# Row factors over partitions by two DMAs instead of matmuls with ones, and a square root moved ahead of a scaling, in a hybrid HGRN2 / RG-LRU layer

## Chip, cores and metric

The kernel runs on one core of a Trainium2 chip. The metric is the device time of one launch in microseconds (us); the median over the runs is given with its lowest and highest value, and one further execution was taken with the hardware profiler. All shapes are float32; many matmul operands are float32r, the packed form in which TensorE multiplies float32 in one pass.

## What is computed

One layer on x of shape (2048, 1024), cut from the reference:

```
xn    = rms_norm(x, mix_norm_w)                 # x / sqrt(mean(x^2) + 1e-6) * w, per row
proj  = xn @ w_in                               # 1024 -> 6 groups of 512 columns
o_hg  = hgrn2(q, f, i, g)                       # 4 heads, chunked gated recurrence
o_lru = rglru(conv(lru_x), lru_gate)            # real-gated linear recurrence
h     = x + concat(o_hg, o_lru) @ w_out         # 1024 -> 1024, "output projection"
hn    = rms_norm(h, ffn_norm_w)
h     = h + (silu(hn @ w_gate) * (hn @ w_up)) @ w_down     # 1024 -> 2816 -> 1024
out   = rms_norm(h, final_norm_w)
```

## The kernel before

**Halves and tiles.** The 2048 rows are done in two halves of 1024, each of two chunks `c` of 512 rows, each of four row tiles `tt` of 128. `KT` is 8 (slices of 128 of the 1024 features), `TPC` is 4, `CW` is 512. Matmul operands are kept as a pair: a rounded "hi" part, made by ScalarE (ACT), and the rest, "lo", made by VectorE (DVE) as a subtraction; three matmuls (hi·hi, hi·lo, lo·hi) stand for one product. So each operand costs a cast on ACT and a subtraction on DVE (`split`, lines 234 and 170 of the profile).

**The second half's input.** In `norm_steps(c)` (lines 621 to 651) the second half's chunk c is normalised while the first half's output projection runs. It has three kinds of steps. Four `stat` steps load row tiles of x and sum their squares on ACT; the last calls `factor`, which makes `rs`, a tile of 128 partitions by 4, with one POOL instruction (L559): the row factors 1/sqrt(mean + eps), a row in a partition. `spread` brings these 512 factors into a tile `row` of 128 partitions by 512, the same 512 numbers in every partition, since the transposed x (`xk`, features in partitions, rows in the free dimension) needs a factor per column. Before, it does so in `row_spread`: four times DVE scales the identity by a column of `rs` (L590, tile `dg`), and TensorE multiplies ones by it (L591, tile `tpb`, in PSUM); ACT copies the result to SBUF (L639). Eight `apply` steps each load a slice `xk` of the transposed x, multiply it on DVE by the weight and by `row` (L646), and split it into `xn` hi and lo.

**The output projection.** It is a seven-product scheme over 2x2 blocks, in the order p1, p2, p6, p5, p7, p3, p4 (`OORDER`). Each product has four row tiles with 12 matmuls each, 48 in all (line 1311), left operands `mx_a`, `mx_b`, `mx_f`, `mx_e`, `mx_g`, `mx_c`, `mx_d`, and two weight tiles `raw_o` loaded by SP and split into `whi_o` and `wlo_o`. The `raw` pool has three buffers, so the load of a weight tile waits until the `wlo` subtraction of the tile three before it has read its buffer. `prepare` makes the next product's left operand on ACT and DVE: sums `s1`, `s2` and differences of `hg` and `y` (line 1237), then `split`. After each row tile DVE adds the bank in PSUM to the residual (`res`, line 1316).

**What sets the order.** The norm steps are hung at numbered slots of the projection: slot 4·i + tt is run after row tile tt of product i; statistics sit at slots -4 to 3, `spread` of chunk c at slot 8 + c, `apply` at 12 + 8·c and on. Within what dependencies allow, the tile framework's scheduler then fixes the order on each engine at build time; on the chip each engine takes its instructions in that order. Buffers come from rotating pools: `xin` (4) holds the x tiles and then `xk`, `late` (5) holds `dg`, `row` and others.

**The end.** In the last product of the last half (p4 of the down projection, lines 1088 to 1091) each row tile g is finished as soon as its sum is there: `square` sums its second half's squares on ACT (L937), takes the root on ACT (L942) and the reciprocal on DVE (L943); `finish` scales one half of the columns on DVE (L957), the other on ACT (L958), and stores both, from SP and, for the last tile, also from ACT's queue (L959, L960).

Of the kernel before, what the change touches and what calls it, by code (L numbers as in the profile page):

```python
# [8 lines left out]
F32 = mybir.dt.float32  # L9
F32R = mybir.dt.float32r  # L10
AF = mybir.ActivationFunctionType
ALU = mybir.AluOpType

P = 128
# [11 lines left out]
TPC = CW // P  # L26
NTT = T // P
# [10 lines left out]
def hybrid_layer(ctx: ExitStack, tc: tile.TileContext, x, x_t, norm_w, cols, w_in, gate_w, w_out, w_gu, w_down, out):  # L38
    nc = tc.nc
# [4 lines left out]
    dram = ctx.enter_context(tc.tile_pool(name="dram", bufs=1, space=bass.MemoryType.DRAM))  # L44
# [7 lines left out]
    def xin(nm):  # L52
        return sb.tile([P, CW], F32, tag="xin", name=nm, bufs=4)


    def block(nm, dt=F32R):
        return sb.tile([P, 4, CW], dt, tag="bt", name=nm, bufs=14)
# [7 lines left out]
    def late(nm):  # L65
        return sb.tile([P, CW], F32, tag="late", name=nm, bufs=5)
# [4 lines left out]
    def aux(nm):  # L71
        return psp.tile([P, CW], F32, tag="aux", name=nm)
# [12 lines left out]
        out=tri[:, 0:P], in_=tri[:, 0:P], pattern=[[1, P]], compare_op=ALU.is_ge, fill=0.0, base=0, channel_multiplier=-1  # L85
# [145 lines left out]
    def split(dst, src, scale=None):  # L231
        if scale is None:
            ins = nc.scalar.copy(out=dst[0], in_=src)  # L233
            v.tensor_tensor(out=dst[1], in0=src, in1=f(dst[0]), op=ALU.subtract)
        else:
            ins = nc.scalar.activation(out=dst[0], in_=src, func=AF.Copy, scale=scale)
            v.scalar_tensor_tensor(out=dst[1], in0=src, scalar=scale, in1=f(dst[0]), op0=ALU.mult, op1=ALU.subtract)
        return ins

    def act_tile(nm):  # L240
        return [[block(f"{nm}_{s}{n}") for n in range(2)] for s in range(2)]

    def part(xt, s, k, ts=slice(0, CW)):
        return xt[s][k // 4][:, k % 4, ts]
# [301 lines left out]
    def chain(ins, behind):  # L546
        tc.add_manual_dep(
            ins.ins,
            behind.ins.name,
            mybir.DependencyInfo(mybir.DependencyClass.NoSync, mybir.DependencyReason.DATA),  # L550
            reason="order",
        )
# [3 lines left out]
    def factor(sums, nm):  # L556
        rs = small.tile([P, 4], F32, tag="ss", name="ss_" + nm, bufs=8)
        v.scalar_tensor_tensor(out=rs, in0=sums[0], scalar=EPS, in1=sums[1], op0=ALU.add, op1=ALU.add)
        nc.gpsimd.tensor_tensor(out=rs, in0=rs, in1=mhalf, op=ALU.pow)  # L559
        return rs  # L560
# [21 lines left out]
                    v.tensor_tensor(out=lo[:, ks], in0=raw[i][:, ks], in1=f(hi[:, ks]), op=ALU.subtract)  # L582
        return xw

    def row_spread(c, rs, nm="x0"):
        nm = f"{nm}_{c}"
        pbc, dg = aux("tpb" + nm), late("dg" + nm)
        for tt in range(TPC):
            ts = slice(tt * P, (tt + 1) * P)
            v.tensor_scalar(out=dg[:, ts], in0=ident, scalar1=rs[:, tt : tt + 1], scalar2=None, op0=ALU.mult)  # L590
            nc.tensor.matmul(pbc[:, ts], lhsT=ones.broadcast_to([P, P]), rhs=dg[:, ts], start=True, stop=True)  # L591
        return pbc
# [28 lines left out]
    def norm_steps(c):  # L621
        box = {}
        sums = []

        def stat(tt):
            if tt == 0:
                sums.extend(small.tile([P, 4], F32, tag="ss", name=f"ss{n}_x1_{c}", bufs=8) for n in range(2))
            r0 = T + c * CW + tt * P
            for n in range(2):
                p = xin(f"x1_{c}_{tt}_{n}")  # L630
                nc.sync.dma_start(out=p, in_=x[r0 : r0 + P, n * CW : (n + 1) * CW])
                nc.scalar.activation(out=p, in_=p, func=AF.Square, scale=1.0 / 32.0, accum_out=sums[n][:, tt : tt + 1])
            if tt == TPC - 1:
                box["rs"] = factor(sums, f"x1_{c}")

        def spread():
            pbc = row_spread(c, box["rs"], "x1")
            box["row"] = late(f"row1_{c}")
            nc.scalar.copy(out=box["row"], in_=pbc)  # L639

        def apply(k):
            if k == 0:
                box["xn"] = act_tile(f"xn1_{c}")
            p = xin(f"xk1_{c}_{k}")
            nc.sync.dma_start(out=p, in_=x_t[k * P : (k + 1) * P, T + c * CW : T + (c + 1) * CW])
            v.scalar_tensor_tensor(  # L646
                out=p, in0=p, scalar=par[:, C_NW + k : C_NW + k + 1], in1=box["row"], op0=ALU.mult, op1=ALU.mult
            )
            split([part(box["xn"], s, k) for s in range(2)], p)

        return box, [lambda tt=tt: stat(tt) for tt in range(TPC)], spread, [lambda k=k: apply(k) for k in range(KT)]


    def tt_(out, a, b, op, e=None):
        (e or v).tensor_tensor(out=out, in0=a, in1=b, op=op)  # L655
# [217 lines left out]
    def residual(half):  # L873
        hp = [[page(f"hd{half}_{g}_{n}") for n in range(2)] for g in range(NTT)]
        return hp
# [5 lines left out]
    def down_plain(half, c, fs, hp, extra, ahead=()):  # L881
# [38 lines left out]
        for tt in range(TPC):  # L920
            finish(half, c * TPC + tt, hp[c * TPC + tt])
# [4 lines left out]
    def final_row(half, g):  # L926
        if g not in fin:
            fin[g] = wvec(2, f"wfin{half}_{g}") if g % TPC == 0 else fin[g - 1]
        return fin[g]

    def square(half, g, n, p):
        first = (half, g) not in sums_f
        if first:
            sums_f[half, g] = small.tile([P, 4], F32, tag="sf", name=f"sf{half}_{g}", bufs=8)
        ss = sums_f[half, g]
        junk = late(f"jf{half}_{g}_{n}")
        nc.scalar.activation(out=junk, in_=p, func=AF.Square, scale=1.0 / 32.0, accum_out=ss[:, n : n + 1])  # L937
        if first:
            v.tensor_scalar(out=ss[:, 2:3], in0=ss[:, n : n + 1], scalar1=EPS, scalar2=None, op0=ADD)
            tt_(p, p, final_row(half, g)[:, n * CW : (n + 1) * CW], MUL)  # L940
        else:
            nc.scalar.activation(out=ss[:, 3:4], in_=ss[:, n : n + 1], func=AF.Sqrt, bias=ss[:, 2:3])  # L942
            v.reciprocal(out=ss[:, 3:4], in_=ss[:, 3:4])  # L943

    def finish(half, g, hp, n=None):
        row = final_row(half, g)
        r0 = half * T + g * P
        if n is None:
            rs = rstd_of(hp, f"f{half}_{g}")
            for n in range(2):  # L950
                nsl = slice(n * CW, (n + 1) * CW)
                v.scalar_tensor_tensor(out=hp[n], in0=hp[n], scalar=rs, in1=row[:, nsl], op0=MUL, op1=MUL)
                nc.sync.dma_start(out=out[r0 : r0 + P, nsl], in_=hp[n])
            return
        rs = sums_f[half, g][:, 3:4]
        nsl, osl = slice(n * CW, (n + 1) * CW), slice((1 - n) * CW, (2 - n) * CW)
        v.scalar_tensor_tensor(out=hp[n], in0=hp[n], scalar=rs, in1=row[:, nsl], op0=MUL, op1=MUL)  # L957
        nc.scalar.activation(out=hp[1 - n], in_=hp[1 - n], func=AF.Copy, scale=rs)  # L958
        nc.sync.dma_start(out=out[r0 : r0 + P, nsl], in_=hp[n])  # L959
        (nc.scalar if g == NTT - 1 else nc.sync).dma_start(out=out[r0 : r0 + P, osl], in_=hp[1 - n])  # L960

    fin = {}

# [141 lines left out]
    for half in range(2):  # L1107
# [3 lines left out]
        if half == 0:  # L1111
            warm_up()
            raw, xs, rows = first_loads()
            xw, rs = [], []
# [59 lines left out]
        for s in range(8):  # L1174
# [6 lines left out]
            for c in range(NC):  # L1181
                k = 2 * (NC * s + c)
                nm = f"{half}_{s}_{c}"
# [13 lines left out]
                else:  # L1197
                    d = {"pre": lru_pre(i, pa, pb, nm)}
                    g = k + 3 if c == 0 else k + 2
# [5 lines left out]
        def at_slot(i, *fs):  # L1205
            fill.setdefault(i, []).extend(fs)

        if half == 0:
            for c in range(NC):
                nb, stats, spread, applies = norm_steps(c)  # L1210
                boxes.append(nb)
                for j, f_ in enumerate(stats):
                    at_slot(-4 + 4 * c + j, f_)
                at_slot(8 + c, spread)
                for j, f_ in enumerate(applies):
                    at_slot(12 + 8 * c + j, f_)
        else:
            bops[0], steps, last = acts(hn_d[0], "0", False)
            for j, f_ in enumerate(steps[0]):
                at_slot(12 + j, f_)  # L1220
            for j, f_ in enumerate(steps[1]):
                at_slot(min(20 + j, 27), f_)
# [17 lines left out]
        for c in range(NC):  # L1240
# [11 lines left out]
            t = block(f"hg{half}_{c}", F32)  # L1252
            hg.append(t)
            for tt in range(TPC):
                tp = transposed(tt, 0, vts[c][:, tt, :], f"o{half}_{c}_{tt}")
                nc.scalar.activation(
                    out=t[:, :, tt * P : (tt + 1) * P], in_=tp, func=AF.Copy, scale=par[:, C_HN : C_HN + 1]
# [34 lines left out]
        for i, name in enumerate(OORDER):  # L1292
# [9 lines left out]
            c, n = to[name]  # L1302
            if i in (1, 2, 5):
                residual_in(*to[OORDER[i + 1]])
            for tt in range(TPC):
# [8 lines left out]
                g = c * TPC + tt  # L1314
                p = res[g, n]
# [63 lines left out]
    for half in range(2):  # L1379
        ffn_up(half, bops[half], later if half == 0 else ())  # L1380
        hp = residual(half)
# [87 lines left out]
```

## Time and profile before

| | |
|---|---|
| median of 3 runs | 2073.01 us (2072.82 to 2073.02) |
| the profiled execution | 2072.78 us, of which the span from first to last instruction is 2071.1 us |
| TensorE clock granted | 0.999 of full speed |
| busy: TensorE / weight loads / DVE / ACT / POOL | 99% / 83% / 75% / 49% / 3% of the span |
| DMA | 279.60 MB, 135 GB/s on the mean; every transfer is issued by SP but two, which ACT issues; none by POOL |

PE is TensorE's matmuls and PEld its weight loads. Matmuls are pipelined: a busy time of one is longer than the step from one start to the next. In a timeline each row has the start, the duration, engine, line, operation, out<-in, the count, and in brackets the idle time ahead of it and what ended it; instructions of one line that follow each other are merged. In a list of waits the columns are total time, times and the longest. Numbers at the end of tile names are left out in the profile.

### The profile page before, as it was taken

How to read it: one execution, taken by the hardware profiler on the slowest of the kernel's cores; microseconds unless marked ns; L12 is line 12 of the kernel's file. 1: busy time of each engine (PE TensorE's matmuls, PEld its weight loads, DVE VectorE, ACT ScalarE, POOL GpSimd, SP SyncE). 2: the span in 40 equal slices, each digit the busy share in tenths (PEclk: the TensorE clock that was granted, in tenths of full speed). 3: DMA queues.
4: the chain of work that ended last, by engine and by line, in shares of the span. 5: the costliest groups of instructions: out<-in, count | busy, mean ns of one | idle time of the engine just before them, and what ended most of it. 6: DMA issues, size and time to landing. Idle time of an engine off the chain costs nothing.

```text
span 2071.1 us, 26057 instructions
## 1 busy us (share of the span) xinstructions
PE 2059.6 (99%) x9570; PEld 1710.8 (83%) x9570; DVE 1555.1 (75%) x2517; ACT 1021.6 (49%) x1698; POOL 68.8 (3%) x97
## 2 busy tenths in 40 slices
PE   9999999999999999999999999999999999999998
PEld 8888887888888888888888888888888888888887
DVE  7878758836888599667667578779776676669787
ACT  7677776456777554343343354245333333344334
POOL 1011110000000000000000000001000000000000
PEclk9999999999999999999999999999999999999999
DMA  7322227841111364433433384356332232266424
GB/s 265 101 78 79 69 77 244 299 123 41 41 41 42 104 231 148 148 127 117 142 127 128 112 303 139 122 162 196 110 118 92 96 129 94 85 247 238 156 85 142
DMA packets 148351, 279.60 MB, mean 135 GB/s; under 512 B 12288, under 2 KB 28672, under 8 KB 148224
## 3 DMA queue, kind: packets, MB, share of 16 engines
q1 hardware_dynamic: 147936, 277.66, 39.5%
q8 instruction: 75, 1.23, 0.2%
q14 instruction: 52, 0.43, 0.1%
q10 hardware_dynamic: 288, 0.29, 0.0%
HBM read 210.53 MB, written 67.37 MB: 134 GB/s over the span
## 4 chain that ended last, share of the span: by engine, by line
PE 96%; ACT 1%; DVE 1%; DMA 1%; issue 0%; POOL 0%; ACTq 0%; DVEq 0%
PE quad_e L771 12%; PE quad_g L771 12%; PE quad_a L771 12%; PE pda L1055 10%; PE pdb L1055 7%; PE quad_f L771 6%; PE pox L1311 4%; PE pa L261 3%; PE pb L262 3%; PE pa L263 3%; PE pb L263 3%; PE pa L262 3%; PE pb L261 3%; PE poyp L1311 3%; PE pv L615 2%; PE pd L911 1%
## 5 line engine op out<-in xcount | busy, mean ns | idle before, releaser
L771 PE MATMUL quad_e<-act_c,wgu_c 128*128 128x512 f32 x528 | 128.7, 391 | 0.0
L771 PE MATMUL quad_e<-act_e,wgu_e 128*128 128x512 f32 x528 | 127.5, 389 | 0.0
L771 PE MATMUL quad_f<-act_f,wgu_f 128*128 128x512 f32 x528 | 127.5, 389 | 0.0
L771 PE MATMUL quad_g<-act_g,wgu_g 128*128 128x512 f32 x528 | 127.5, 389 | 0.0
L771 PE MATMUL quad_a<-act_a,wgu_a 128*128 128x512 f32 x528 | 127.5, 390 | 0.0
L771 PE MATMUL quad_a<-act_b,wgu_b 128*128 128x512 f32 x528 | 127.1, 390 | 0.3 <-ACT e L808 0.3
L771 PE MATMUL quad_g<-act_d,wgu_d 128*128 128x512 f32 x528 | 127.2, 390 | 0.0
L771 PEld LDWEIGHTS quad_a<-act_b,wgu_b 128*128 128x128 f32 x528 | 99.2, 188 | 21.1 <-ACT e L808 0.6
L771 PEld LDWEIGHTS quad_a<-act_a,wgu_a 128*128 128x128 f32 x528 | 99.2, 188 | 20.7 <-ACT wgu_a L233 0.3
L771 PEld LDWEIGHTS quad_g<-act_g,wgu_g 128*128 128x128 f32 x528 | 99.2, 188 | 20.5
L771 PEld LDWEIGHTS quad_f<-act_f,wgu_f 128*128 128x128 f32 x528 | 99.2, 188 | 20.5
L771 PEld LDWEIGHTS quad_e<-act_e,wgu_e 128*128 128x128 f32 x528 | 99.2, 188 | 20.5
L771 PEld LDWEIGHTS quad_g<-act_d,wgu_d 128*128 128x128 f32 x528 | 99.2, 188 | 20.3
L771 PEld LDWEIGHTS quad_e<-act_c,wgu_c 128*128 128x128 f32 x528 | 99.2, 188 | 20.2
L655 DVE TENSOR_TENSOR u<-u,quad_g 128x512 f32<-128x512 f32 x88 | 60.3, 686 | 59.2 <-PE quad_g L771 59.2
L261 PE MATMUL pa<-xn,whi_in 128*128 128x512 f32 x256 | 101.0, 395 | 0.0
L263 PE MATMUL pa<-xn,whi_in 128*128 128x512 f32 x256 | 100.7, 394 | 0.0
L262 PE MATMUL pb<-xn,wlo_in 128*128 128x512 f32 x256 | 100.6, 393 | 0.0
L263 PE MATMUL pb<-xn,whi_in 128*128 128x512 f32 x256 | 100.6, 393 | 0.0
L262 PE MATMUL pa<-xn,wlo_in 128*128 128x512 f32 x256 | 100.5, 393 | 0.0
L261 PE MATMUL pb<-xn,whi_in 128*128 128x512 f32 x256 | 100.2, 391 | 0.0
L293 ACT ACT_TABLE_LOAD x74 | 94.9, 1283 | 2.5 <-PEq L1458 1.2
(379 smaller groups left out, 4893.5 us busy)
## 6 DMA issues: line engine op xcount, KB each, us to landing
raw<-in_w_gu SPq DMA_DIRECT2D x88, 512.0 KB, 3.8
raw_in<-in_w_in SPq DMA_DIRECT2D x47, 512.0 KB, 4.2
ao_p<-as SPq DMA_DIRECT2D x76, 256.0 KB, 2.5
xk<-in_x_t SPq DMA_DIRECT2D x32, 256.0 KB, 5.3
x<-in_x SPq DMA_DIRECT2D x32, 256.0 KB, 4.5
res<-in_x SPq DMA_DIRECT2D x32, 256.0 KB, 6.2
raw_o_p<-wo_p SPq DMA_DIRECT2D x16, 512.0 KB, 4.7
h<-res SPq DMA_DIRECT2D x32, 256.0 KB, 4.0
```

Source lines behind the costliest of these rows:

```text
L261: nc.tensor.matmul(ps, lhsT=whi[:, ks], rhs=hi, start=(k == 0), stop=False)
L262: nc.tensor.matmul(ps, lhsT=wlo[:, ks], rhs=hi, start=False, stop=False)
L263: nc.tensor.matmul(ps, lhsT=whi[:, ks], rhs=lo, start=False, stop=(k == KT - 1))
L293: in_line(lambda: nc.scalar.preload_act_table(func))
L615: ins = nc.tensor.matmul(banks[tt], lhsT=a, rhs=w, start=(k + i == 0), stop=(k == KT - 1 and i == 2))
L655: (e or v).tensor_tensor(out=out, in0=a, in1=b, op=op)
L771: nc.tensor.matmul(ps, lhsT=w[:, s, ks], rhs=x, start=first and k + n == 0, stop=k == 3 and n == 2, skip_group_check=not first)
L911: nc.tensor.matmul(ps, lhsT=a[:, 1, tsl], rhs=whi[:, nsl], start=False, stop=(i == len(fs) - 1))
L1055: nc.tensor.matmul(ps, lhsT=x, rhs=y, start=first and q + n == 0, stop=q == gr.n - 1 and n == 2, skip_group_check=not first)
L1311: nc.tensor.matmul(ps, lhsT=x_, rhs=y_, start=first and q + m == 0, stop=q == 3 and m == 2, skip_group_check=not first)
```

## The change

Two parts. In `norm_steps`, `spread` no longer calls `row_spread`: POOL issues a DMA that writes the 128 x 4 factors, transposed, as 4 x 128 into DRAM (512 elements of 4 bytes), and then a DMA that reads these 512 numbers back into every partition of `row`. The `spread` slots become 4 and 6 in place of 8 and 9. In the end part, ACT's scaling of a tile's other half (and its store) is held back until the next tile's root is on ACT, and ordered behind it.

```diff
-    def row_spread(c, rs, nm="x0"):
-        nm = f"{nm}_{c}"
-        pbc, dg = aux("tpb" + nm), late("dg" + nm)
+    def row_spread(c, rs):
+        pbc, dg = aux(f"tpbx0_{c}"), late(f"dgx0_{c}")
...
         def spread():
-            pbc = row_spread(c, box["rs"], "x1")
+            d = dram.tile([TPC, P], F32, name=f"rs1_{c}")
             box["row"] = late(f"row1_{c}")
-            nc.scalar.copy(out=box["row"], in_=pbc)
+            nc.gpsimd.dma_start(out=d.rearrange("t p -> p t"), in_=box["rs"])
+            nc.gpsimd.dma_start(out=box["row"], in_=d.rearrange("t p -> (t p)").partition_broadcast(P))
...
-            nc.scalar.activation(out=ss[:, 3:4], in_=ss[:, n : n + 1], func=AF.Sqrt, bias=ss[:, 2:3])
+            roots[half, g] = nc.scalar.activation(out=ss[:, 3:4], in_=ss[:, n : n + 1], func=AF.Sqrt, bias=ss[:, 2:3])
...
-        nc.scalar.activation(out=hp[1 - n], in_=hp[1 - n], func=AF.Copy, scale=rs)
         nc.sync.dma_start(out=out[r0 : r0 + P, nsl], in_=hp[n])
-        (nc.scalar if g == NTT - 1 else nc.sync).dma_start(out=out[r0 : r0 + P, osl], in_=hp[1 - n])
-
-    fin = {}
+        def other():
+            ins = nc.scalar.activation(out=hp[1 - n], in_=hp[1 - n], func=AF.Copy, scale=rs)
+            if g < NTT - 1:
+                chain(ins, roots[half, g + 1])
+            (nc.scalar if g == NTT - 1 else nc.sync).dma_start(out=out[r0 : r0 + P, osl], in_=hp[1 - n])
+
+        if n == 1:
+            nc.scalar.activation(out=hp[0], in_=hp[0], func=AF.Copy, scale=rs)
+            nc.sync.dma_start(out=out[r0 : r0 + P, osl], in_=hp[0])
+        else:
+            waiting.append(other)
+            if g == NTT - 1:
+                for f_ in waiting:
+                    f_()
+            elif len(waiting) > 1:
+                waiting.pop(0)()
+
+    fin, roots, waiting = {}, {}, []
...
-                at_slot(8 + c, spread)
+                at_slot(4 + 2 * c, spread)
```

The scheduler draws other conclusions from these lines, so the order on the engines moves around them. Three places matter.

**DVE, in p1 of the first half's output projection, before.** `mx_b1` is the lo part of p2's left operand, `wlo_o0_p1_1` that of p1's second weight tile, `ss_x1_1` the second chunk's sums, `v0_1` the gated values that TensorE transposes next.

```order
L1249 TENSOR_TENSOR v0_1_487<-v0_1_487,sg0_1_2_2971 128x512
L234 TENSOR_TENSOR mx_b1_0_2871<-y0_0_676,mx_b0_0_2870 128x1024 x2
L170 TENSOR_TENSOR wlo_o0_p1_1_3063<-raw_o0_p1_1_3060,whi_o0_p1_1_3062 128x1024
L558 SCALAR_TENSOR_TENSOR ss_x1_1_3156<-ss0_x1_1_3091,ss1_x1_1_3092 128x4
L1249 TENSOR_TENSOR v0_1_487<-v0_1_487,sg0_1_3_3005 128x512
```

The same place now:

```order
L1263 TENSOR_TENSOR v0_1_487<-v0_1_487,sg0_1_2_2971 128x512
L234 TENSOR_TENSOR mx_b1_0_2871<-y0_0_676,mx_b0_0_2870 128x1024
L646 SCALAR_TENSOR_TENSOR xk1_0_0_3380<-xk1_0_0_3380,par_99,row1_0_3210 128x512
L234 TENSOR_TENSOR mx_b1_0_2871<-y0_0_676,mx_b0_0_2870 128x1024
L170 TENSOR_TENSOR wlo_o0_p1_1_3063<-raw_o0_p1_1_3060,whi_o0_p1_1_3062 128x1024
L558 SCALAR_TENSOR_TENSOR ss_x1_1_3156<-ss0_x1_1_3091,ss1_x1_1_3092 128x4
```

The first multiplication by `row1_0` has come up between the two halves of `mx_b1`; before, it stood behind p5's operands. It waits for two transfers: `xk1_0_0` and `row1_0`.

**DVE, in p2, before.** `s2` and `hg0_1` are made for p6 and p7, `mx_f1` is the lo part of p6's left operand.

```order
L1237 TENSOR_TENSOR s2_0_3172<-s1_0_3171,hg0_0_2839 128x1024
L1237 TENSOR_TENSOR hg0_1_3017<-hg0_0_2839,hg0_1_3017 128x1024
L1316 TENSOR_TENSOR res0_3_0_3048<-res0_3_0_3048,pox_3_0_3053 128x512
L1237 TENSOR_TENSOR s2_0_3172<-s1_0_3171,hg0_0_2839 128x1024
L1237 TENSOR_TENSOR hg0_1_3017<-hg0_0_2839,hg0_1_3017 128x1024
L1316 TENSOR_TENSOR res0_0_0_3042<-res0_0_0_3042,poyp2_0_0_3183 128x512
L1237 TENSOR_TENSOR y0_0_676<-y0_0_676,s2_0_3172 128x1024
L170 TENSOR_TENSOR wlo_o0_p6_1_3168<-raw_o0_p6_1_3165,whi_o0_p6_1_3167 128x1024
L234 TENSOR_TENSOR mx_f1_0_3178<-s2_0_3172,mx_f0_0_3177 128x1024
```

The same place now:

```order
L1251 TENSOR_TENSOR s2_0_3172<-s1_0_3171,hg0_0_2839 128x1024
L1251 TENSOR_TENSOR hg0_1_3017<-hg0_0_2839,hg0_1_3017 128x1024
L646 SCALAR_TENSOR_TENSOR xk1_0_1_3398<-xk1_0_1_3398,par_99,row1_0_3210 128x512
L1330 TENSOR_TENSOR res0_3_0_3048<-res0_3_0_3048,pox_3_0_3053 128x512
L646 SCALAR_TENSOR_TENSOR xk1_0_2_3416<-xk1_0_2_3416,par_99,row1_0_3210 128x512
L1251 TENSOR_TENSOR s2_0_3172<-s1_0_3171,hg0_0_2839 128x1024
L1251 TENSOR_TENSOR hg0_1_3017<-hg0_0_2839,hg0_1_3017 128x1024
L646 SCALAR_TENSOR_TENSOR xk1_0_3_3434<-xk1_0_3_3434,par_99,row1_0_3210 128x512
L1330 TENSOR_TENSOR res0_0_0_3042<-res0_0_0_3042,poyp2_0_0_3183 128x512
L1251 TENSOR_TENSOR y0_0_676<-y0_0_676,s2_0_3172 128x1024
L170 TENSOR_TENSOR wlo_o0_p6_1_3168<-raw_o0_p6_1_3165,whi_o0_p6_1_3167 128x1024
L234 TENSOR_TENSOR mx_f1_0_3178<-s2_0_3172,mx_f0_0_3177 128x1024
```

Three multiplications by `row1_0` have moved ahead of `mx_f1`.

**TensorE, at the start of p6, before** (`pox` and `poyp5` are banks in PSUM):

```order
L1311 MATMUL pox_2_0_3052<-whi_o0_p6_0_3161,mx_f0_0_3177 128x512
L1311 MATMUL pox_2_0_3052<-wlo_o0_p6_0_3162,mx_f0_0_3177 128x512
L591 MATMUL tpbx1_0_3294<-dgx1_0_3295,ones_95 128x128 x4
L1311 MATMUL pox_3_0_3053<-whi_o0_p6_0_3161,mx_f0_0_3177 128x512
L1311 MATMUL pox_3_0_3053<-wlo_o0_p6_0_3162,mx_f0_0_3177 128x512
L1311 MATMUL pox_0_0_3050<-whi_o0_p6_0_3161,mx_f1_0_3178 128x512
```

The same place now:

```order
L1325 MATMUL pox_2_0_3052<-whi_o0_p6_0_3161,mx_f0_0_3177 128x512
L1325 MATMUL pox_2_0_3052<-wlo_o0_p6_0_3162,mx_f0_0_3177 128x512
L1325 MATMUL pox_3_0_3053<-whi_o0_p6_0_3161,mx_f0_0_3177 128x512
L1325 MATMUL pox_3_0_3053<-wlo_o0_p6_0_3162,mx_f0_0_3177 128x512
L1325 MATMUL poyp5_0_0_3359<-whi_o0_p5_0_3261,mx_e0_0_3271 128x512
L1325 MATMUL pox_0_0_3050<-whi_o0_p6_0_3161,mx_f1_0_3178 128x512
```

The matmuls with ones are gone, and one matmul of p5 has come up in front of the first that needs `mx_f1`. Behind it, 25 more matmuls follow before the first that needs `wlo_o0_p5_0`, the lo part of p5's first weight tile; in p1, seven matmuls of row tile 3 now stand ahead of the first that needs `wlo_o0_p1_1`.

## The prediction, made before the changed kernel was run

> **What bounds the kernel now.** The page comes first: TensorE is busy for all but 11.5 us of the span.
>
> ```profile
> span 2071.1 us, 26057 instructions
> PE 2059.6 (99%) x9570; PEld 1710.8 (83%) x9570; DVE 1555.1 (75%) x2517; ACT 1021.6 (49%) x1698; POOL 68.8 (3%) x97
> ```
>
> So the edit can win what TensorE spends or waits for at its two places, and no more. The list of TensorE's waits shows that the first place has one:
>
> ```profile
> PE tpbx L591 <- DVE dgx L590: 1.4, 1, 1.4
> ...
> PE pox L1311 <- DVE mx_f L234: 0.5, 1, 0.5
> ```
>
> Both are waits for DVE, so the table by stretches (length, then PE, PEld, DVE, ACT, POOL, clock, DMA share, GB/s) is next:
>
> ```profile
> 320.00:330.00 10.00, 10.00 (x48) 8.27 (x47) 5.72 (x8) 7.89 (x13) 1.01 (x1) 1.00 1.03 398
> 340.00:350.00 10.00, 9.51 (x45) 7.42 (x44) 10.00 (x11) 5.45 (x7) 0.00 (x0) 1.00 0.45 159
> ```
>
> At 320 the DMA engines are full (398 GB/s); at 340 DVE has no gap while TensorE has some. TensorE's timeline there:
>
> ```profile
> 322.01 0.39 PE L1311 MATMUL pox<-wlo_o_p,mx_a 128*128 128x512 f32 x1
> ...
> 339.49 0.39 PE L1311 MATMUL pox<-whi_o_p,mx_f 128*128 128x512 f32 x1
> ...
> 340.62 0.39 PE L1311 MATMUL pox<-wlo_o_p,mx_f 128*128 128x512 f32 x1
> 340.85 1.05 PE L591 MATMUL tpbx<-dgx,ones 128*128 128x128 f32 x8
> ...
> 342.83 0.72 PE L1311 MATMUL pox<-whi_o_p,mx_f 128*128 128x512 f32 x2 [0.47 <-DVE mx_f L234]
> ...
> 359.23 0.40 PE L1311 MATMUL poyp<-wlo_o_p,mx_e 128*128 128x512 f32 x1
> ```
>
> Five matmuls of p6 take 340.62 - 339.49, so a step is 0.226 us. And DVE's:
>
> ```profile
> 317.45 2.36 DVE L234 TENSOR_TENSOR mx_b<-y,mx_b 128x1024 fp32r<-128x1024 f32 x2
> 319.72 1.22 DVE L170 TENSOR_TENSOR wlo_o_p<-raw_o_p,whi_o_p 128x1024 fp32r<-128x1024 f32 x1
> ...
> 341.56 1.22 DVE L234 TENSOR_TENSOR mx_f<-s,mx_f 128x1024 fp32r<-128x1024 f32 x1
> 342.69 0.68 DVE L1316 TENSOR_TENSOR res<-res,poyp 128x512 f32<-128x512 f32 x1
> 343.29 1.22 DVE L1237 TENSOR_TENSOR y<-y,s 128x1024 f32<-128x1024 f32 x1
> ...
> 354.36 2.73 DVE L646 SCALAR_TENSOR_TENSOR xk<-xk,par,row 128x512 f32<-128x512 f32 x4
> ```
>
> From start to start a 1024-wide subtraction takes (319.72 - 317.45)/2 = 1.135 us, a `res` 0.60; an `xk` takes 2.73/4 = 0.68.
>
> **Removed: 4.6 us.** From p6's first matmul (339.49) to the twentieth of p5 (359.23) lie 67 matmuls: 48 of p6, twelve and five of p5 ahead of the second group with ones, two behind. 67 x 0.226 = 15.1 us; it took 19.74. The 4.6 us are two groups of eight short matmul passes with ones, the waits for `dgx` (1.4) and for `mx_f1` (0.5), and slower steps beside them. ACT's two copies and DVE's scalings of the identity go too; the first group of these lies in DVE's idle time, the second behind everything counted below, so I cost them at nothing.
>
> **Added: DVE's queue is longer ahead of what TensorE needs.** The first `xk` now stands between the halves of `mx_b1`, which DVE reaches at 317.45 + 1.135 = 318.6. What it waits for:
>
> ```profile
> 309.75 1.01 POOL L559 TENSOR_TENSOR ss_x<-ss_x,tinies 128x4 f32<-128x4 f32 x1 [8.94 <-DVE ss_x L558]
> ```
> ```profile
> 315.61 0.33 SPq L645 DMA_DIRECT2D xk<-in_x_t  x1
> ...
> 320.97 0.33 SPq L163 DMA_DIRECT2D raw_o_p<-wo_p  x1
> ```
> ```profile
> DMA to landing us min/median/max: 4.4/4.4/4.4
> ```
>
> The last line is that `xk`'s: it lands at 315.61 + 4.4 = 320.0, so DVE idles 1.4 us even if `row` is there. `row` needs two transfers in a row, from 310.76. The trace has none from POOL; between 296 and 345 these are the nearest, SP's loads of 256 KB before and after the DMA engines fill up:
>
> ```profile
> x<-in_x SPq DMA_DIRECT2D x16, 256.0 KB, 3.1
> res<-in_x SPq DMA_DIRECT2D x16, 256.0 KB, 6.3
> ```
>
> From below, two of 3.1 us: 317.0. From above, two of 6.3 and 1 us of POOL (its own instruction's time) for each: 325.4. I take 3.1 for the tiny write, since the engines still have room then, 4.4 for the read, as for the `xk` issued at that time, and 1 us of POOL for each: 320.3. Price: TensorE needed p1's second `wlo` at 322.01; seven matmuls now stand ahead of it, so at 322.01 + 1.58 = 323.6. DVE delivers it 0.68 + 2 x 1.135 = 2.95 us, and some 0.1 to the reader, after the `xk` can start. So up to 320.55 the wait costs nothing; the cover is those seven matmuls, and beyond it each us costs one. [...]
>
> What waits for DVE there: SP's load of p6's first weight tile, held until that `wlo` has read the buffer. It was issued at 320.97 (DVE: 319.72 + 1.22) and will be at about 323.3. The DMA queues are backed up, so it lands when the bytes ahead of it have: one `res` tile more has moved in front of it, 256 KB at 398 GB/s, 0.66 us. ACT's cast of it was
>
> ```profile
> 327.87 1.05 ACT L169 CAST whi_o_p<-raw_o_p 128x1024 fp32r<-128x1024 f32 x1 [1.59 <-DMA raw_o_p<-wo_p]
> ```
>
> and so ends at 328.92 + 0.66, and DVE's `wlo` of it starts at 329.6. From there to the end of the first `mx_f1`, DVE's queue now holds ten 1024-wide instructions (`wlo` twice, `s1` twice, `s2` twice, `hg` twice, `y`, `mx_f1`), four `res` and three `xk`: 11.35 + 2.4 + 2.04 = 15.8 us, with no gap. `mx_f1` is ready at 345.4, against 342.8 before. TensorE has p6's eight matmuls and one of p5 to do until 339.49 + 9 x 0.226 = 341.5, and then **waits 3.9 us** in place of 0.5. From below: no delay of the load, 3.2; from above: `row`'s own 256 KB too, 4.5.
>
> Behind it TensorE has 26 matmuls (5.9 us) until `wlo` of p5, and DVE five 1024-wide (`mx_e1` twice, `y`, `mx_g1`, `wlo`) and two `res`, 6.9 us: **another 1.0 us**. After that DVE has all of p5 and p6 for a lead, with no group of identities, and I see nothing late: behind the waiting read on POOL's queue stands only the second chunk's factor, and `row1_1` is used from slot 20 on, in p3. Sum: 3.9 + 1.0 - 4.6 = **+0.3 us** (-0.4 to +0.9).
>
> **The end: -0.2 us.** ACT's timeline, and its last store:
>
> ```profile
> 2065.41 0.19 ACT L937 ACTIVATION_READ_ACCUMULATOR jf<-hd 128x1 f32 x1
> 2065.50 0.71 ACT L958 ACTIVATE hd<-hd,sf 128x512 f32<-128x512 f32 x1
> 2066.11 0.28 ACT L942 ACTIVATE sf<-sf 128x1 f32<-128x1 f32 x1
> 2066.62 0.72 ACT L958 ACTIVATE hd<-hd,sf 128x512 f32<-128x512 f32 x1 [0.23 <-DVE sf L943]
> 2067.37 0.38 ACTq L960 DMA_DIRECT2D out_h<-hd  x1
> ```
> ```profile
> out_h<-hd ACTq DMA_DIRECT2D x1, 256.0 KB, 2.8
> ```
>
> The root can start at about 2065.63, 0.48 earlier. But ACT then does both scalings behind it: 2065.63 + 0.2 + 0.61 + 0.72 = 2067.16 against 2067.34, so the last store leaves 0.2 us earlier. DVE's half gains 0.48; the neighbour's store goes out 0.3 later, closer to the two last. Bounds: 0 and -0.5; I take -0.2, the step of the queue that issues last.
>
> Against the profiled execution (2072.78, of which 2071.1 is span) that is +0.1; the median of the runs is 2073.01. Forecast: 2073.1 us, from 2072.1 to 2073.9 by these bounds.
>
> **Rivals.** (A) *The row comes late.* By the upper price `row` lands at 325.4, DVE stands 4.8 us past the cover of 320.55, TensorE waits as long for p1's `wlo`, and p6's weight load, issued as much later, loses its place in a queue by then shorter: 2073.1 + 4.8 + 0.5 = 2078.4. It turns the result slower by over 0.2% (4.1 us, about what a measurement can tell from no change) from 324.5 on. For it: three steps that no row shows, 512 elements of 4 bytes among them. Against it: the load at 310 to 320 is lighter than what 6.3 was measured in. [...] 0.12 for this, and 0.13 for a `row` between 320.9 and 324.5, which gives up to 2077.
>
> (B) *DVE is not late for p6*, since its idle time in p1 (5.72 of 10.00 us busy from 320 to 330) takes up the `xk`. Then the 4.6 go and only the second wait or none replaces them: 2073.0 - 4.6 - 0.2 = 2068.2 at best. Against it: the three `xk` stand behind the `wlo` that is bound by the load, in a stretch where DVE shows 10.00 of 10.00. 0.05.
>
> (C) The forecast: 0.70.
>
> **Numbers.** The range reaches into both sides: from 2071.2 (part of B) to 2076.5 (most of the middle case of A). Chances: faster 0.04, same 0.84, slower 0.12.
>
> **What would show it.** Right: TensorE's waits list has no `tpbx`, but about 4 us for `mx_f` and 1 us for a `wlo_o_p` or the cast behind it; DVE's first `xk` with `row` starts near 320.2 after about 1.5 us idle, released by a DMA. Wrong: a wait of TensorE in p1 (A), or `mx_f1` ending before 344 (B).

## The result and the profile after

The changed kernel takes 2083.32 us (median of 6 runs, 2081.83 to 2084.29) against 2073.02 us (6 runs, 2072.82 to 2073.26) beside it: a ratio of 1.0051, 95% interval 1.0041 to 1.0061, slower by 10.3 us. The profiled execution took 2083.97 us, 2081.9 of it span. The forecast of 2073.1 (2071.2 to 2076.5) missed.

The loss lies in the out-projection of the first half. TensorE's first and last matmul of it, in the timeline of before and then of after:

```profile
316.66 0.48 PE L1311 MATMUL pox<-whi_o_p,mx_a 128*128 128x512 f32 x1
...
398.25 0.39 PE L1311 MATMUL pox<-whi_o_p,mx_d 128*128 128x512 f32 x1
```
```profile
316.37 0.48 PE L1325 MATMUL pox<-whi_o_p,mx_a 128*128 128x512 f32 x1
...
409.29 0.39 PE L1325 MATMUL pox<-whi_o_p,mx_d 128*128 128x512 f32 x1
```

It took 81.6 us and takes 92.9: 11.3 more, all of the loss and more. TensorE's waits from 300 to 420 us, after (total, times, longest):

```profile
PE pox L1325 <- ACT mx_f L233: 3.7, 1, 3.7
PE pox L1325 <- DVE wlo_o_p L170: 3.0, 1, 3.0
PE pox L1325 <- ACT sg L295: 2.0, 1, 2.0
PE pox L1325 <- ACT whi_o_p L169: 1.1, 1, 1.1
```

9.8 us, where before had the 1.9 that the prediction shows. Three of the four name ACT, for which the prediction's sum has TensorE wait nowhere. What ACT and DVE were waiting for, in their timelines after:

```profile
320.35 0.63 ACT L631 ACTIVATE x<-x 128x512 f32<-128x512 f32 x1 [3.02 <-DMA x<-in_x]
...
349.64 1.05 ACT L169 CAST whi_o_p<-raw_o_p 128x1024 fp32r<-128x1024 f32 x1 [13.05 <-DMA raw_o_p<-wo_p]
350.59 1.04 ACT L233 CAST mx_f<-s 128x1024 fp32r<-128x1024 f32 x1
```
```profile
327.41 0.75 DVE L646 SCALAR_TENSOR_TENSOR xk<-xk,par,row 128x512 f32<-128x512 f32 x1 [9.37 <-DMA row<-rs]
...
347.02 0.75 DVE L646 SCALAR_TENSOR_TENSOR xk<-xk,par,row 128x512 f32<-128x512 f32 x1 [4.02 <-DMA xk<-in_x_t]
```

Every one is a DMA, and not only the new ones: `x`, `xk` and `raw_o` are loads that before had too. POOL's timeline shows when the new ones were issued:

```profile
310.44 0.94 POOL L638 DMA_DIRECT2D rs<-ss_x  x1 [0.31 <-POOL ss_x L559]
320.66 0.57 POOL L639 DMA_DIRECT2D row<-rs  x1 [9.28 <-DMA rs<-ss_x]
```

The first is the store of the 512 factors, the second the read back, 10.2 us later. Beside it the DMA view from 300 to 325 us, before and then after: the busy tenths of the DMA engines and the GB/s in 40 slices of 0.625 us, and after also the median time to landing of the transfers issued there.

```profile
DMA  9579995988849956675289971579993799999999
GB/s 364 167 184 305 328 272 167 324 229 259 308 148 285 331 200 177 252 203 213 33 262 334 295 285 59 79 249 295 154 82 98 282 367 370 397 416 377 390 410 423
```
```profile
DMA  7499777958979594852989959344262344959999
GB/s 279 105 331 377 203 275 288 223 226 262 292 262 347 161 272 134 233 210 75 293 257 243 98 29 23 16 16 23 52 82 82 98 108 72 85 239 324 393 347 354
...
raw_o_p<-in_w_out SPq DMA_DIRECT2D x1, 512.0 KB, 10.5
xk<-in_x_t SPq DMA_DIRECT2D x1, 256.0 KB, 9.6
row<-rs POOLq DMA_DIRECT2D x1, 256.0 KB, 6.7
rs<-ss_x POOLq DMA_DIRECT2D x1, 2.0 KB, 9.6
```

From the 23rd to the 35th slice (313.8 to 321.9 us) all DMA engines together move 16 to 108 GB/s, part of the time while they count as busy; in the same slices of before they move 59 to 397. The store of 2 KB, issued at 310.44, is on its way until 320.0; soon after, the pace is back. The `xk` load takes 9.6 us where it took 4.4. So one small store seems to delay the loads of that stretch. The second chunk's, issued at 332.43, is no better; the DMA view of after from 325 to 350 us:

```profile
rs<-ss_x POOLq DMA_DIRECT2D x1, 2.0 KB, 14.2
```

What TensorE's clock did, in stretches of 10 us (length, busy time of PE, PEld, DVE, ACT, POOL, granted clock, DMA share, GB/s), after:

```profile
320.00:330.00 10.00, 4.39 (x16) 2.39 (x14) 2.59 (x3) 8.37 (x14) 0.57 (x1) 0.83 0.88 298
330.00:340.00 10.00, 9.51 (x38) 7.86 (x39) 8.04 (x10) 1.86 (x3) 2.23 (x2) 0.83 0.91 236
340.00:350.00 10.00, 8.03 (x36) 6.32 (x34) 5.98 (x8) 0.36 (x1) 0.56 (x1) 1.00 0.97 204
350.00:360.00 10.00, 8.31 (x24) 6.07 (x25) 10.00 (x12) 10.00 (x13) 0.00 (x0) 0.66 0.61 222
```

From 350 to 360 it is busy for 8.31 us and does only 24 matmuls: behind a wait it runs slowly for a while. An estimate of what that costs is busy time times the missing clock: 4.39 x 0.17 + 9.51 x 0.17 + 8.31 x 0.34 = 5.2 us. The waits grew by 9.8 - 1.9 = 7.9. The matmuls with ones are gone, which is worth 2.7 us, the prediction's 4.6 less the 1.9 of waits in it. Together: 7.9 + 5.2 - 2.7 = 10.4 of the 11.3.

### The profile page after: what moved, and what is told of

Its sections match the earlier page's. It is cut to its first block, busy times and chain, and to the rows that moved or that the text cites. A ratio compares the mean times of both kernels' runs of the same rounds, so it can differ in the third digit from the quotient of the medians.

```text
span 2081.9 us, 26036 instructions
## 1 busy us (share of the span) xinstructions
PE 2062.5 (99%) x9554; PEld 1710.0 (82%) x9554; DVE 1553.2 (75%) x2509; ACT 1021.2 (49%) x1696; POOL 72.6 (3%) x101
## 4 chain that ended last, share of the span: by engine, by line
PE 95%; DVE 1%; ACT 1%; DMA 1%; SPq 0%; issue 0%; ACTq 0%; DVEq 0%
PE quad_e L771 12%; PE quad_g L771 12%; PE quad_a L771 12%; PE pda L1069 9%; PE pdb L1069 7%; PE quad_f L771 6%; PE pox L1325 3%; PE pa L261 3%; PE pa L263 3%; PE pb L262 3%; PE pb L263 3%; PE pa L262 3%; PE pb L261 3%; PE poyp L1325 3%; PE pv L614 2%; PE pg L273 1%
```

## The experiments

Theory 1 was that the transposed store holds up the loads; theory 2, that DVE standing behind `row` in its queue makes the loss; theory 3, that POOL's way of issuing is the cost. A fourth comes up on the way: that any transfer of POOL's in this stretch costs something. The kernels called ghost add to the kernel before only a store that nobody reads. Ratios are to the kernel before on the same chip, with 95% intervals.

**The end part alone (tail_only).** The hunks at the end of the diff, on the kernel before.

> The end part of the change alone, on the kernel before. Every theory of the lost 10 us places them in the out-projection of the first half, so all expect 0.2 us less than before (0 to 0.5 less): about 2072.8 us. If the end part carried any of the loss, this kernel would be slower than before.

2072.73 us against 2072.61, 0.9999 (0.999 to 1.0008): it carries none of the loss. Its last tile in ACT's timeline:

```profile
2065.38 0.19 ACT L937 ACTIVATION_READ_ACCUMULATOR jf<-hd 128x1 f32 x1
...
2067.15 0.35 ACTq L963 DMA_DIRECT2D out_h<-hd  x1
```

1.77 us from the sum to the last store, against the 1.96 (2065.41 to 2067.37) of before: the forecast's 0.2 us, too little for the runs to resolve.

**The store alone (ghost).**

```diff
                 box["rs"] = factor(sums, f"x1_{c}")
+                d = dram.tile([TPC, P], F32, name=f"rs1_{c}")
+                nc.gpsimd.dma_start(out=d.rearrange("t p -> p t"), in_=box["rs"])
```

> The kernel before, with the transposed store of the 512 factors to DRAM added on POOL for both chunks, and nobody who reads it; the order on all other engines is that of before. Theory 1 (the 512 elements of 4 bytes hold up the DMA engines, so that loads of x and of weights land late): TensorE waits for silu outputs (sg) and for the cast of a weight tile in p1 and for mx_f at p6, together 4 to 8 us, so 2077 to 2081 us. Theory 2 (the loss comes only from DVE, which stands in its queue before the first xk until the row has come): no wait is added, 2073 us within 1 us.

2083.73 us, 1.0051 (1.0037 to 1.0065): a store that nobody waits for costs 11.1 us, with the order of all other engines as before. Theory 2 falls as an account of the 10 us. (Ghost still does the matmuls with ones. After is slower by about as much without them, so some 4 us more are lost in it, which no run takes apart.) Its waits, what ACT waited for, and the landing of its two stores:

```profile
PE pox L1313 <- ACT mx_f L233: 5.3, 1, 5.3
PE pox L1313 <- ACT whi_o_p L169: 2.6, 1, 2.6
```
```profile
321.76 0.63 ACT L632 ACTIVATE x<-x 128x512 f32<-128x512 f32 x1 [4.06 <-DMA x<-in_x]
...
346.78 1.04 ACT L169 CAST whi_o_p<-raw_o_p 128x1024 fp32r<-128x1024 f32 x1 [12.67 <-DMA raw_o_p<-wo_p]
```
```profile
DMA to landing us min/median/max: 10.7/11.5/12.4
```

**The multiplications later on DVE, the DMAs of after (xk_late).**

```diff
+            if c == 0:
+                chain(ins, lo_of["p5", 0])      # ins: xk times row; lo_of: DVE's last lo of p5's operand
```

> The kernel after, with the multiplications of the first chunk's xk ordered behind the lo part of p5's operand on DVE, which is where they stood before; both DMAs stay. Theory 1: DVE no longer waits for the row, so the 3 us wait for the second wlo in p1 goes, but x, weights and xk still land late: 2076 to 2080 us. Theory 2 (only DVE's place in the queue costs): the matmuls with ones are gone and nothing replaces them, 2068 to 2070 us.

2084.46 us, 1.0058 (1.0042 to 1.0073), no better than after. In the trace the four multiplications stand right behind p5's operand, which is still seven instructions ahead of their place in before (there they follow `mx_g` and a `wlo`). DVE no longer stands behind `row` in p1, but the weight tiles that TensorE needs next come from the same stalled transfers, by way of ACT's casts. The two longest of its waits:

```profile
PE pox L1330 <- ACT mx_f L235: 6.7, 1, 6.7
PE pox L1330 <- ACT whi_o_p L169: 3.2, 1, 3.2
```

So taking DVE from behind `row` won nothing; another load was as late.

**The factors stored as they lie (contig).**

```diff
-            d = dram.tile([TPC, P], F32, name=f"rs1_{c}")
+            d = dram.tile([P, TPC], F32, name=f"rs1_{c}")
-            nc.gpsimd.dma_start(out=d.rearrange("t p -> p t"), in_=box["rs"])
+            nc.gpsimd.dma_start(out=d, in_=box["rs"])
...
-                out=p, in0=p, scalar=..., in1=box["row"], ...
+                out=p.rearrange("q (t p) -> q t p", t=TPC), ..., in1=box["row"].rearrange("q (p t) -> q t p", t=TPC), ...
```

> The kernel after, with the factors stored to DRAM as they lie, 16 bytes in a piece from each of 128 partitions in place of 512 single elements of 4 bytes, and DVE reading the row with a stride of 4 elements so that the columns meet their factors; the instruction order is that of after. Theory 1 (the number of small pieces): the store takes 3 to 4 us in place of 9.6 and 14.2, other loads keep their pace, and the time is 2071 to 2075 us. Theory 3 (a DMA issued by POOL costs this whatever its pieces): no change from after, 2083 us.

2077.04 us, 1.0023 (1.0013 to 1.0032). The two stores land in 4.0 and 6.3 us, so POOL's issuing alone is not the cost (theory 3); 4.4 us of loss stay, 2 more than expected. TensorE's three waits (in its timeline), DVE's queue ahead of the last of them, and DVE's 16 multiplications by `row`, 1150 ns each against 746 in before, because of the stride:

```profile
325.06 0.50 PE L1326 MATMUL pox<-wlo_o_p,mx_a 128*128 128x512 f32 x1 [1.65 <-DVE wlo_o_p L170]
...
344.85 0.47 PE L1326 MATMUL poyp<-whi_o_p,mx_e 128*128 128x512 f32 x1 [1.80 <-DVE res L1331]
348.16 1.22 PE L1326 MATMUL pox<-whi_o_p,mx_f 128*128 128x512 f32 x2 [2.84 <-DVE mx_f L234]
```
```profile
331.04 1.23 DVE L170 TENSOR_TENSOR wlo_o_p<-raw_o_p,whi_o_p 128x1024 fp32r<-128x1024 f32 x1 [2.49 <-ACT whi_o_p L169]
...
346.86 1.24 DVE L234 TENSOR_TENSOR mx_f<-s,mx_f 128x1024 fp32r<-128x1024 f32 x1
348.00 0.71 DVE L1331 TENSOR_TENSOR res<-res,poyp 128x512 f32<-128x512 f32 x1
```
```profile
L646 DVE SCALAR_TENSOR_TENSOR xk<-xk,par,row 128x512 f32<-128x512 f32 x16 | 18.2, 1150 | 4.3 <-DMA xk<-in_x_t 4.3
```

All three waits are now for DVE: but for the stride, this is the case that the prediction described.

**Both cures (contig_late).** contig with xk_late's line.

> Both cures at once: the factors are stored as they lie (pieces of 16 bytes, as in contig) and the first chunk's xk are multiplied behind p5's operand (as in xk_late). Theory 1 (the small pieces hold up the other loads; DVE's queue is only the second cost): weights land nearly on time, the 4.6 us of the matmuls with ones are gone, p6's wait for mx_f is 0 to 1.5 us instead of 2.8, and the time is 2068 to 2072 us, faster than before. Theory 4 (any transfer of POOL in this stretch costs what contig still shows): no change from contig, about 2077 us.

2075.61 us, 1.0016 (1.0007 to 1.0025): above theory 1's range, and, with intervals that overlap, not shown to differ from contig. With DVE's order changed, the scheduler lets some of p5 in among p6 on TensorE, and other waits take the place of p6's:

```profile
PE poyp L1331 <- DVE res L1336: 2.1, 1, 2.1
PE poyp L1331 <- ACT whi_o_p L169: 1.8, 1, 1.8
PE pox L1331 <- DVE mx_f L236: 0.6, 1, 0.6
```

**What in the store is dear (five more ghosts).** First the queue and the number of pieces: the same store from SP; the store as it lies; and one column of it, in its transposed place.

```diff
-                nc.gpsimd.dma_start(out=d.rearrange("t p -> p t"), in_=box["rs"])
+                nc.sync.dma_start(out=d.rearrange("t p -> p t"), in_=box["rs"])                    # ghost_sp
+                nc.gpsimd.dma_start(out=d, in_=box["rs"])                                          # ghost_contig, d is [P, TPC]
+                nc.gpsimd.dma_start(out=d.rearrange("t p -> p t")[:, 0:1], in_=box["rs"][:, 0:1])  # ghost_col
```

> The kernel before with ghost's transposed store of 512 elements issued by SP, whose queue carries all other loads, in place of POOL's. SP's order changes at three places, by one DMA each. If the pieces are the cost: 9 us or more to landing, and 2080 to 2086 us, with the loads behind it in SP's queue late as well. If the queue that POOL issues through is the cost: landing in 2 to 4 us and 2073 to 2075 us.

2082.39 us, 1.0047 (1.0034 to 1.0061). The first store's landing, from 300 to 325 us:

```profile
rs<-ss_x SPq DMA_DIRECT2D x1, 2.0 KB, 8.7
```

The second takes 14.5. The queue makes no difference that matters; theory 3 falls.

> The kernel before with the store that nobody reads, as it lies: 128 pieces of 16 bytes. If the number of pieces decides: it lands in 4 to 6 us, TensorE waits 0 to 2 us more than before, 2073 to 2076 us. If any such store from POOL costs the same: as ghost, 2084 us.

2073.26 us, 1.0003 (0.9994 to 1.0012), landing:

```profile
DMA to landing us min/median/max: 3.3/4.7/6.0
```

Free, as far as the runs can tell.

> The kernel before with a store that nobody reads, of one column of the factors only: 128 elements of 4 bytes, a quarter of ghost's. If the number of pieces decides, it is as ghost_contig: lands in 4 to 6 us, 2073 to 2076 us. If the store's bytes being written element by element (4 in place of 16 bytes) is dearer by itself, it is worse than ghost_contig, up to 2080 us.

2081.43 us, 1.004 (1.0026 to 1.0053), landing:

```profile
DMA to landing us min/median/max: 9.2/10.3/11.3
```

As many pieces as ghost_contig, a quarter of its bytes, and nearly the whole loss. So the number of pieces is not it either, and that form of theory 1 fell. Left were the element of 4 bytes by itself (1b), or writes from many partitions that lie close together in DRAM (1a: in ghost_col all 128 within 512 bytes). Two more ghosts keep single elements of 4 bytes and move them apart:

```diff
+                d = dram.tile([P, TPC, P], F32, name=f"rs1_{c}")                # ghost_512: all 512
+                nc.gpsimd.dma_start(out=d[:, :, 0], in_=box["rs"])
...
+                d = dram.tile([P, TPC], F32, name=f"rs1_{c}")                   # ghost_16: one column
+                nc.gpsimd.dma_start(out=d[:, 0:1], in_=box["rs"][:, 0:1])
```

> The kernel before with a store that nobody reads: all 512 factors, element by element as in ghost, but each to a DRAM address of its own 512 bytes from the next. Theory 1a (what costs is that many small writes from different partitions fall into the same short stretch of DRAM and wait for each other): landing in 2 to 4 us, no pace lost by the other loads, 2073 us within 1 us. Theory 1b (an element of 4 bytes is dear by itself, wherever it goes): as ghost, 10 to 14 us to landing and 2081 to 2085 us.

2073.20 us, 1.0002 (0.9993 to 1.0011), landing:

```profile
DMA to landing us min/median/max: 3.3/4.4/5.5
```

> The kernel before with a store that nobody reads: the 128 factors of one column, as in ghost_col, but 16 bytes apart in DRAM instead of 4. By theory 1a it is as ghost_contig, since as many writes fall into each stretch: landing in 4 to 6 us and 2073 to 2075 us. By theory 1b it is as ghost_col: 9 to 11 us to landing and 2080 to 2083 us.

2073.09 us, 1.0001 (0.9992 to 1.001), landing:

```profile
DMA to landing us min/median/max: 3.6/4.6/5.6
```

Both free. The same 512 single elements cost 11 us when they lie 4 bytes apart in DRAM with neighbours from different partitions, and nothing 512 bytes apart; 128 of them cost 8.6 us at a pitch of 4 bytes and nothing at 16. So 1b falls, and the place in DRAM decides, as 1a says. That the writes wait for each other there is not shown; nor do these runs tell whether the pitch decides, or how many writes fall into a stretch of some length.

**Towards a faster kernel (contig_later, rows4).** First, against contig_late, xk at the place it had before the change; then, against contig_later, other rows in a partition, with which DVE reads `row` without the stride (that hunk isn't shown).

```diff
-                chain(ins, lo_of["p5", 0])
+                chain(ins, lo_of["o0_p5_1"])                                    # contig_later
...
-                nc.sync.dma_start(out=p, in_=x[r0 : r0 + P, n * CW : (n + 1) * CW])
+                rows = x[r0 : r0 + CW, n * CW : (n + 1) * CW].rearrange("(p t) d -> p t d", t=TPC)
+                nc.sync.dma_start(out=p, in_=rows[:, tt, :])                    # rows4, in stat; r0 = T + c * CW
```

> As contig_late (factors stored as they lie), with the first chunk's xk multiplied still later on DVE, behind the lo part of p5's second weight tile, the place it had before the change. If DVE's queue ahead of p5 and p7 made the 4.5 us of waits that contig_late still shows: waits of 0 to 2 us in the out-projection, 2069 to 2073 us. If the waits come from TensorE's own order, which lets some of p5 in ahead of p6: 2074 to 2077 us, as contig_late.

2071.86 us, 0.9996 (0.9987 to 1.0004): the loss is gone, a gain not shown. Theory 4 falls too, since POOL's transfers are those of contig.

> As contig_later, but the statistics' row tiles are loaded so that partition p holds rows 4p to 4p+3; then the factors as they lie are already in the order of the columns, 16 bytes from each partition, and DVE reads the row without a stride. The order of the instructions is that of contig_later. DVE's multiplications by the row go back from 1.13 to 0.75 us, 6 us less for the 16 of them, in a stretch in which DVE has no gap. If that DVE time was behind the remaining waits: 2069.5 to 2071.5 us, faster than before. If it lies in DVE's lead over TensorE: 2071.5 to 2072.5 us, as contig_later.

2069.89 us against 2073.08, 0.9988 (0.9979 to 0.9997): faster by 3.2 us. Its only wait in the out-projection, DVE's 16 multiplications, and the last matmul:

```profile
PE poyp L1331 <- ACT whi_o_p L171: 1.0, 1, 1.0
```
```profile
L649 DVE SCALAR_TENSOR_TENSOR xk<-xk,par,row 128x512 f32<-128x512 f32 x16 | 11.6, 742 | 1.3 <-DMA xk<-in_x_t 1.1
```
```profile
394.82 0.39 PE L1331 MATMUL pox<-whi_o_p,mx_d 128*128 128x512 f32 x1
```

The multiplications are back at 742 ns. The first matmul is at 316.48, so the out-projection takes 78.3 us, 3.3 less than before. That rows4 is faster than contig_later (timed on another chip) is not shown: their intervals overlap.

## Why the prediction was wrong

**Removed, 4.6 us: right.** rows4 has no group of ones; its out-projection is 3.3 us shorter, with a wait of 1.0 in their place: 4.3.

**The row at 320.3: the step that failed.** "I take 3.1 for the tiny write, since the engines still have room then" priced 512 elements as a small load. It took 9.6 us, the read 6.7 against 4.4, and `row` was there at 327.4, past even the upper end of 325.4. The bounds came from loads of 256 KB, and I took a transfer of 2 KB to be no dearer than those; ghost and ghost_512 show that its place in DRAM decides, and not the number of elements: 512 of them land in 10.7 and 12.4 us in ghost, in 3.3 and 5.5 in ghost_512. With the store as it lies (contig, 4.0 and 5.7 us) the row comes about 321.1, near the 320.3.

**A transfer priced alone.** Worse, the sum let the store delay only what waits for it. In ghost nobody waits and 11 us are lost: while it is on its way, loads of x and of weights land late (`xk` in 10.5 us against 4.4 in before, a weight tile in 11.4 against 5.9). The sum put that at nothing, without a reason.

**p6's wait of 3.9 us.** After shows 3.7 at this place, for another reason: ACT's cast of a weight tile that had waited 13.05 us for its load. In contig, where loads are nearly on time (`xk` in 5.7 us, a weight tile in 6.6), TensorE does wait here for DVE: 1.8 for the `res` that empties p5's bank and, one matmul of p5 later, 2.8 for `mx_f`, 4.6 together. From p6's `wlo` to the end of `mx_f` DVE takes 348.00 - 331.04 = 17.0 us, which is the sum's 15.8 and 1.2 for the stride in three `xk`. So the mechanism stands, and DVE's queue was counted right; but its start was 1.4 us too early (329.6 against 331.04), since the weight tile landed later than the 0.66 us in the sum. The second wait (1.0 for a `wlo` of p5) is not there.

**The clock after a wait: not priced.** I let each us of waiting cost one. In after the waits' 9.8 us brought some 5.2 of slow matmuls with them, by the estimate above.

**Rival A** had the sign and the place (a wait in p1 for `wlo`), but its price, 5.3 us, was half of the loss, since it was the row alone. POOL's issuing is not the cause: it issued the store at 310.44, where the sum has 310.76, and the same store from SP lands as late, in 8.7 and 14.5 us against ghost's 10.7 and 12.4.

**The end: right**, -0.2 us by the trace.

## What to carry over

Before a tiny DMA is put into a stretch with full queues, look at where its pieces land: here single elements from many partitions, 4 bytes apart in DRAM, held up the loads beside them (ghost 11.1 us slower, ghost_col 8.6), while the same elements 512 bytes apart, 128 of them 16 bytes apart, or pieces of 16 bytes cost nothing that the runs could tell (1.0002, 1.0001, 1.0003). Choose the layout upstream so that what a partition holds is already contiguous in the target (rows4 gets this by changing which rows a partition loads). And price such waits of TensorE as after's at more than themselves: its 9.8 us of waits brought an estimated 5.2 us of slow matmuls, while behind contig_later's wait of 1.6 the clock stayed at 1.00.

## What the runs showed of the hardware

A store of 2 KB (after, ghost, ghost_sp), or of 0.5 KB (ghost_col), in elements 4 bytes apart took 8.7 to 14.5 us. All of the core's DMA traffic fell meanwhile, for some slices of 0.625 us to 16 GB/s in after and to 7 in ghost, with the store on POOL's queue, and to 20 or less in ghost_sp, with the store on SP's.

In after TensorE's granted clock fell to 0.50 twice in the stretch with its waits and was back at 1.00 after 6.8 us. The matmuls behind the wait of 3.66 us, with a step of 0.43 us in place of 0.226:

```profile
351.68 0.79 PE L1325 MATMUL pox<-whi_o_p,mx_f 128*128 128x512 f32 x1 [3.66 <-ACT mx_f L233]
352.28 0.63 PE L1325 MATMUL pox<-wlo_o_p,mx_f 128*128 128x512 f32 x1
352.70 0.63 PE L1325 MATMUL pox<-whi_o_p,mx_f 128*128 128x512 f32 x1
```

By the trace, the granted clock is 0.50 from 326.6 to 333.4 us and from 350.5 to 357.3 in after, and from 323.1 to 326.5 and from 347.0 to 353.8 in ghost: 6.8 or 3.4 us at a time.

How long a wait has to be for the clock to drop is not shown. In ghost the first drop came in a wait of 2.6 us; in contig_late the waits were 2.1, 1.8 and 0.6 us long, and the clock is 0.83 from 350 to 360 us; in contig_later it stayed at 1.00 behind one of 1.6 us that ended at 342.6. Nor did the drop always come in the wait or at its end: in after the clock dropped at 326.6, though the wait of 2.0 us had ended at 325.2. The tables by stretches of ghost and then contig_later:

```profile
320.00:330.00 10.00, 7.41 (x29) 5.69 (x28) 2.08 (x3) 6.96 (x13) 1.83 (x2) 0.83 0.77 267
```
```profile
340.00:350.00 10.00, 8.38 (x37) 6.59 (x36) 10.00 (x11) 6.12 (x8) 0.00 (x0) 1.00 0.45 160
```

A product on DVE of 128x512 that reads one operand with a stride of 4 elements took 1150 ns in contig, in place of 746 in before.
